# A hybrid mixer and product-key expert layer on one core: one-hot building paced by halves of first products, and a dense schedule with two blocks' sums resident in PSUM

## The chip, the core and the metric

The kernel runs on one core of one Trainium2 chip. The core's engines work side by side, each through a queue of its own in order: TensorE (PE in the profile, its weight loads PEld), VectorE (DVE), ScalarE (ACT), GpSimd (POOL) and SyncE (SP, which here only issues transfers). They are tied to each other by semaphores. The metric is the device time of one execution in microseconds (us); lower is better. Times of three runs stand beside one profiled execution, from which every duration is read.

## The reference, cut to what matters

One layer over 1024 tokens of width 1024. A front part (normalisation, input projection, an RG-LRU group and an S5 group, output projection) makes the residual stream h; the change does not touch it. The second half is the product-key expert layer:

```python
def block(xb):                                   # 128 tokens
    q = (xb @ wq).reshape(128, 8, 256)           # 8 heads
    s1 = einsum('thd,kd->thk', q[..., :128], k1) # 128 keys each
    s2 = einsum('thd,kd->thk', q[..., 128:], k2)
    v1, i1 = top_k(s1, 16); v2, i2 = top_k(s2, 16)
    cand = (v1[..., :, None] + v2[..., None, :]).reshape(128, 8, 256)
    sc, cidx = top_k(cand, 16)
    e = i1[cidx // 16] * 128 + i2[cidx % 16]     # one of 16384 experts
    g = softmax(sc)
    act = gelu(einsum('thkd,td->thk', u_tab[e], xb))
    return einsum('thk,thkd->td', g * act, v_tab[e])
h = h + block(...)
return rms_norm(h, normf_g)
```

## The kernel before

The 8 blocks of 128 tokens are treated in two ways.

**Three gathered blocks (5, 6, 7).** For each chosen expert one row of `peer_u` and later one row of `peer_v` is fetched by an indirect transfer that GpSimd issues (`ask`, L1257), and VectorE takes it in: a product with its sum for a row of u (`gather`, L1296; the profile's `row<-row,xg`), a multiply-add into `hb` for a row of v (L1310; `hb<-row,act,hb`). One block has 128 + 128 rows, so there are 768 rows in all, counted by `mg.units`. Eight buffers hold rows on the way. `finish` (L1315) normalises a gathered block behind its last row and stores it.

**Five dense blocks (0 to 4).** All 16384 experts are computed for these 640 tokens, 128 experts at a time, which is one *tile* j (128 tiles):
- *First product* (`first`, L1335): gelu(u_j x) for 640 tokens, as two halves of 320 tokens. A half is 8 x 3 matmuls into one PSUM bank (`ap`; every float32 operand is split into a high and a low part, hence three products) and one ScalarE gelu. The operands `uh` and `ul` of a tile are made by ScalarE and VectorE from the loaded `ur`. Each `uh`, `ul` has two buffers.
- *Weights* G: which experts a token chose, and with what weight. `topk` (L1109) finds on VectorE, for one block, the 16 best keys of each half and head, the 16 best sums, their softmax and the two indices. `build_g` (L1197) transposes these into `kt` and then, for each *group* of 4 tokens (32 groups a block, 160 in all), makes one-hots (`ohA` on VectorE; `ohB`, one quarter on VectorE and three on ScalarE), multiplies them on TensorE (`gp`), and copies the result to `gs` on ScalarE. Each 32 tokens `gs` (2 MB) is stored to DRAM as `G_d`.
- *Second product* (`second`, L1489): (G x gelu) times v_j, 24 matmuls for one block of 128 tokens and 4 tiles, or 6 for one block and one tile, in the order `hh vl`, `hl vh`, `hh vh` for each half of 512 columns.

**The stages of the second half.** (1) Queries, and the search for the gathered blocks. (2) The *building stage*: four Python generators are merged by `Merge.run` (L98). It keeps an estimated end time for each engine and thread and lets the thread with the earliest time emit next; a thread that yields a function waits until that is true. The threads are `build` (search and one-hots of one dense block after the other), `ahead` (L1408: the first products of 97 tiles, stored as `A_d` through three `hr` buffers), and the gathers, which may take in rows until 363 of them are done (`gate`, L1279, with `EARLY`). What the merge emits is one fixed order for each engine. (3) `prologue` (L1526), then the *dense stage* (`dense`, L1577): 32 chunks of 4 tiles, in an order that is written out by hand (`manual_schedule`). A chunk does the first product of one tile of the next chunk (the other three were made ahead and are loaded back as `hr`), and the second product of its own 4 tiles for all 5 blocks; on VectorE it splits and weighs the next tiles and takes in a share of the rows that are left. `rows_of(slot)` (L1483) puts that share at seven places, in the proportions `SLOTS`.

In a chunk before, VectorE's parts that the prediction speaks of are: `low_h` and `low_v` (L1383, L1387: the low parts `hl` and `vl` of a tile), `weigh` (L1368: `hr<-hr,gq`), `split_u` (`ul`), and `add` (L1497), which adds a finished pair of PSUM banks (`vp`) to a block's accumulator `acc`:

```python
def add(b, p_):
    V.tensor_tensor(acc[b], acc[b], p_.rearrange("p a b -> p (a b)"), ALU.add)
def pair():
    return ppv.tile([P, 2, 512], F32, name="vp", tag="vp")
```

PSUM has eight banks. In the dense stage two hold `ap`, two the sum of block 4 over all chunks (`total`), and four are two pairs for blocks 0 to 3. TensorE's order in a chunk is: both halves of the first product; block 0; block 1; then, tile by tile, blocks 2, 3 and 4. There are four adds in each chunk. `last` (L1660) finishes the last chunk and normalises the five blocks.

Of the kernel before, what the change touches and what calls it, by code (L numbers as in the profile page):

```python
# [18 lines left out]
P = 128  # L19
# [956 lines left out]
EARLY = 363  # L976


def peer(tc, a, cst, pools, h, nx, mg):
# [129 lines left out]
    def topk(b):  # L1109
# [52 lines left out]
        t1 = pk.tile([P, P], F32, name="t1", tag="t1")  # L1162
# [33 lines left out]

    def build_g(b):  # L1197
        i1, i2, g = yield from topk(b)
        p_ = pt("gt")
        for n, x in enumerate((i1, i2, g.rearrange("p h k -> p (h k)"))):  # L1200
            PE.transpose(p_[:, n * P:(n + 1) * P], x, ident)
        yield
        kt = pk2.tile([P, 5, P], F32, name="kt", tag="kt", bufs=1)
        V.tensor_copy(kt[:, 0:3], p_[:, :3 * P].rearrange("p (a b) -> p a b", b=P))
        V.tensor_scalar(kt[:, 3:5], kt[:, 1:3], -1.0, None, ALU.mult)
        if b == dblocks[-1]:
            mg.flag("k")
        yield
        last = None

        def flush():
            gs, t4, p_ = last
# [15 lines left out]
        for t4 in range(0, P, 4):  # L1228
# [15 lines left out]
            yield  # L1244
# [4 lines left out]
            last = gs, t4, p_  # L1249
            yield  # L1250
        flush()
        yield
# [26 lines left out]
    def gate():  # L1279
        return lambda: mg.units < (share[0] if share else EARLY)  # L1280

    held = []
# [125 lines left out]
    def ahead():  # L1408
        fetch_u()
        yield  # L1410
        while made[0] < NA:
# [38 lines left out]
    def build():  # L1450
        for b in dblocks:
            yield from build_g(b)
        mg.flag("g")

    pace[0] = PACE
    mg.add([(0.0, build()), (1.0, ahead())])
# [120 lines left out]
    def dense():  # L1577
# [3 lines left out]
        for c in range(nch):  # L1581
# [10 lines left out]
            if carry:  # L1592
                add(*carry)
# [14 lines left out]
            load_v(c + 1, 2)  # L1608
# [3 lines left out]

            if more:
                nx[0].turn()
# [3 lines left out]
            add(0, pr[0])  # L1618
            if not more:
                last(now, pr)  # L1620
                return
            rows_of(2)

            pr.append(pair())
            for jj, t in enumerate(now):
                second(pr[2], 2, t, jj == 0, jj == JC - 1)
                if jj == 0:
                    second(total, 4, t, c == 0, False)
                    add(1, pr[1])
                    nx[0].weigh()  # L1630
                    rows_of(3)
                    pr.append(pair())
                second(pr[3], 3, t, jj == 0, jj == JC - 1)
                if jj:
                    second(total, 4, t, False, False)
                if jj:
# [7 lines left out]
                    if jj == 3:  # L1644
                        weights(c + 2) if c + 2 < nch else None
                        add(2, pr[2])
# [10 lines left out]
            carry = 3, pr[3]  # L1657
            now = nx

    def last(now, pr):  # L1660
# [4 lines left out]
        def norm(b):  # L1665
# [6 lines left out]
            else:  # L1672
                for i in range(2):
                    xi = x[:, 512 * i:512 * i + 512]
                    V.tensor_tensor(xi, xi, total[:, i], ALU.add)
# [21 lines left out]
        next(g[0])  # L1697
        rows_of(2)
        p0 = pr[1]
        for b in (2, 3):  # L1700
            p_ = pair()
            for jj, t in enumerate(now):
                second(p_, b, t, jj == 0, jj == JC - 1)
            add(b - 1, p0)
# [8 lines left out]
        for _ in g[2]:  # L1713
            pass
# [95 lines left out]
```

## Time and profile before

| | |
|---|---|
| three runs | 2625.11 us median (2624.61 to 2631.12) |
| the profiled execution | 2620.74 us, its span 2619.0 us |
| busy over the span | PE 96%, DVE 90%, ACT 50%, POOL 43% |
| granted TensorE clock, mean | 0.985 |
| moved by the DMA engines | 753.31 MB, mean 288 GB/s |

The page cuts the span into 40 slices and gives a digit (tenths) of busy time for each:

```profile
## 2 busy tenths in 40 slices
PE   7998999998999999999999999999999999999997
PEld 6776889998999999999999888888888888888885
DVE  7898659998999999999999399999989999999997
ACT  6566434332683965938739643333444433333442
POOL 0000000343664756848547054555445555554551
```

A slice is 65 us. Slices 9 to 22 are the building stage: ACT swings between 3 and 9, since the one-hots of a block come in one burst and the search of the next block stands between two bursts. DVE is at 9 throughout but for one slice near the end (3), in which no row may be taken in any more. From slice 23 on the dense stage runs: PE at 9 in every slice. A busy PE is not PE at its peak, so the prediction goes by the distance from one start to the next, not by these digits.

### The profile page before, as it was taken

To read this page: it belongs to the slowest core of one execution; us is meant where nothing else is said; L and a number is where in the kernel's file an instruction comes from. 1 tells how busy PE (TensorE), PEld (TensorE's weight loads), DVE (VectorE), ACT (ScalarE), POOL (GpSimd) and SP (SyncE) were. 2 spreads that over 40 slices of the span, in tenths; PEclk is the share of its full clock that TensorE was granted. 3 is DMA by queue.
4 is the path that set the end of the run, shared out by engine and by line. 5 is a ranking of instruction groups with operands and counts; after the bars stand their busy time and mean duration, and the time that the engine had idled before them with its cause. 6 is when DMAs were issued, how large, how long until landed. Compare 5 with 4: busy or idle time off the path is not lost.

```text
span 2619.0 us, 40771 instructions
## 1 busy us (share of the span) xinstructions
PE 2503.9 (96%) x14623; PEld 2268.0 (87%) x14623; DVE 2365.3 (90%) x4556; ACT 1321.8 (50%) x2402; POOL 1130.8 (43%) x777
## 2 busy tenths in 40 slices
PE   7998999998999999999999999999999999999997
PEld 6776889998999999999999888888888888888885
DVE  7898659998999999999999399999989999999997
ACT  6566434332683965938739643333444433333442
POOL 0000000343664756848547054555445555554551
PEclk9999999999999999999999999999999999999999
DMA  5113124587899998999989899999989999999993
GB/s 183 30 43 108 61 91 137 189 287 285 305 394 310 360 388 307 397 344 349 399 297 377 277 336 343 346 343 342 342 321 346 344 342 341 343 347 341 340 339 132
DMA packets 302539, 753.31 MB, mean 288 GB/s; under 512 B 28928, under 2 KB 127424, under 8 KB 297600
## 3 DMA queue, kind: packets, MB, share of 16 engines
q0 software_dynamic: 110592, 402.70, 42.2%
q1 hardware_dynamic: 186048, 337.85, 36.4%
q10 hardware_dynamic: 5696, 10.15, 1.2%
q8 instruction: 115, 1.88, 0.3%
q14 instruction: 88, 0.72, 0.1%
HBM read 663.44 MB, written 85.98 MB: 286 GB/s over the span
## 4 chain that ended last, share of the span: by engine, by line
PE 62%; DVE 22%; DMA 7%; ACT 4%; issue 3%; ACTq 0%; SPq 0%; DVEq 0%
PE vp L146 26%; PE ap L146 17%; PE total L146 7%; PE qp L146 4%; DMA A_d<-aa 3%; PE gp L146 3%; PE wop L146 3%; DVE row L146 2%; DVE oh L146 2%; DVE ul L146 2%; DVE hb L146 2%; ACT ohB L146 1%; DVE ix L146 1%; DVE ci L146 1%; DVE v L146 1%
## 5 line engine op out<-in xcount | busy, mean ns | idle before, releaser
L1264 POOL DMA_INDIRECT row<-in_peer_u_dram,idx x384 | 564.8, 1471 | 958.5 <-DVE scv L146 471.0
L1264 POOL DMA_INDIRECT row<-in_peer_v_dram,idx x384 | 563.2, 1467 | 440.6 <-DVE hb L146 302.4
L146 PE MATMUL ap<-xDl,uh 128*128 128x320 f32 x2048 | 650.9, 318 | 14.3 <-ACT aa L146 12.0
L146 PE MATMUL ap<-xDh,ul 128*128 128x320 f32 x2048 | 642.8, 314 | 8.8 <-DVE ul L146 8.8
L146 PE MATMUL ap<-xDh,uh 128*128 128x320 f32 x2048 | 641.5, 313 | 0.0
L146 DVE SCALAR_TENSOR_TENSOR hb<-row,act,hb 128x1024 f32<-128x1024 f32 x384 | 491.5, 1280 | 4.6
L146 DVE CUSTOM_DVE_ANT_0 row<-row,xg 128x1024 f32<-128x1024 f32 x384 | 457.6, 1218 | 7.1 <-DMA row<-in_peer_u_dram,idx 6.6
L146 PE MATMUL vp<-vl,hh 128*128 128x512 f32 x1024 | 400.2, 391 | 9.4 <-DVE h L146 6.7
L146 PEld LDWEIGHTS ap<-xDl,uh 128*128 128x128 f32 x2048 | 390.4, 191 | 17.7 <-ACT aa L146 13.7
L146 PEld LDWEIGHTS ap<-xDh,ul 128*128 128x128 f32 x2048 | 390.5, 191 | 11.9 <-DVE ul L146 10.5
L146 PE MATMUL vp<-vh,hl 128*128 128x512 f32 x1024 | 400.2, 391 | 0.0
L146 PE MATMUL vp<-vh,hh 128*128 128x512 f32 x1024 | 399.0, 390 | 0.0
L146 PEld LDWEIGHTS ap<-xDh,uh 128*128 128x128 f32 x2048 | 389.8, 190 | 0.0
L146 ACT ACTIVATE gq<-gt 128x640 f32<-128x640 f32 x128 | 174.9, 1366 | 306.5 <-DVE hr L146 302.8
L146 PEld LDWEIGHTS vp<-vl,hh 128*128 128x128 f32 x1024 | 192.6, 188 | 50.4 <-DVE h L146 7.6
L146 PEld LDWEIGHTS vp<-vh,hh 128*128 128x128 f32 x1024 | 192.8, 188 | 40.9
L146 PEld LDWEIGHTS vp<-vh,hl 128*128 128x128 f32 x1024 | 192.5, 188 | 38.8
L146 ACT ACTIVATE ohB<-ohB,kt 128x128 f32<-128x128 f32 x480 | 205.3, 496 | 0.0
L146 ACT ACTIVATE aa<-ap 128x320 f32<-128x320 f32 x194 | 84.4, 436 | 237.2 <-PE ap L146 206.0
L146 PE MATMUL gp<-ohB,ohA 128*128 128x128 f32 x1280 | 183.7, 278 | 17.9 <-ACT gs L146 8.9
L146 DVE TENSOR_TENSOR h<-h,vp 128x1024 f32<-128x1024 f32 x128 | 155.7, 1217 | 48.8 <-PE vp L146 48.5
L146 PEld LDWEIGHTS gp<-ohB,ohA 128*128 128x128 f32 x1280 | 169.7, 192 | 22.2 <-ACT gs L146 9.7
(444 smaller groups left out, 4485.9 us busy)
## 6 DMA issues: line engine op xcount, KB each, us to landing
ur<-in_uT_dram SPq DMA_DIRECT2D x128, 512.0 KB, 6.6
vr<-in_peer_v_dram SPq DMA_DIRECT2D x128, 512.0 KB, 6.7
gt<-G_d SPq DMA_DIRECT2D x32, 1280.0 KB, 9.5
G_d<-gs SPq DMA_DIRECT2D x19, 2048.0 KB, 23.5
A_d<-aa SPq DMA_DIRECT2D x96, 320.0 KB, 7.5
hr<-A_d SPq DMA_DIRECT2D x96, 320.0 KB, 5.5
wqr<-in_wq_dram SPq DMA_DIRECT2D x31, 512.0 KB, 3.8
row<-in_peer_u_dram,idx POOLq DMA_INDIRECT x384, 7.4
```

Source lines behind the costliest of these rows:

```text
L146: return fn(*args, **kw)
L1264: G.indirect_dma_start(out=r, out_offset=None, in_=a["peer_v" if at >= P else "peer_u"], in_offset=bass.IndirectOffsetOnAxis(ap=idx[n][:, ...
```

## The change

**In the building stage** the search and the one-hots become two threads. `choose` runs `topk` for all dense blocks and, from the second block on, may take its k-th step only when so many groups are built; `kt` gets two buffers. `build` makes the groups of all blocks in one loop, and a group may be emitted only when the count of *steps* (halves of first products, counted in `ahead`) is at least 23 plus the groups built. Rows are tied to the same count: 64 at first (`FIRST`), then 1.55 more for each half, and 2.1 for each half in the last part (`STEP`). A scratch tile of the search (`t1`) now lies on `ri`.

**In the dense stage** blocks 3 and 4 both keep their sums in PSUM over all chunks (`total`, two pairs of banks), and one pair is left for blocks 0, 1 and 2. There are three adds in each chunk. TensorE's order becomes: first half of the first product; block 0; second half; block 1; then, tile by tile, blocks 3, 4 and 2. `SLOTS` changes, and `last` is rewritten.

```diff
-EARLY = 363
+FIRST, STEP, KT, LEAD = 64, (1.55, 2.1), 2, 23
...
-        t1 = pk.tile([P, P], F32, name="t1", tag="t1")
+        t1 = ri.bitcast(F32)
...
-    def build_g(b):
-        i1, i2, g = yield from topk(b)
...
+    kts, groups, steps = {}, [0], [0]
+
+    def choose():
+        for n, b in enumerate(dblocks):
+            steps = topk(b)
+            k = 0
+            while True:
+                try:
+                    next(steps)
+                except StopIteration as e:
+                    i1, i2, g = e.value
+                    break
+                k += 1
+                at = P // 4 * (n - 1) + k
+                yield lambda: groups[0] >= at
...
+            kts[b] = kt
+            mg.flag(f"k{b}")
+            yield
+        mg.flag("k")
+
+    def build():
...
-        for t4 in range(0, P, 4):
+        for b, t4 in [(b, t4) for b in dblocks for t4 in range(0, P, 4)]:
+            if t4 == 0:
+                if f"k{b}" not in mg.flags:
+                    yield f"k{b}"
+                kt = kts.pop(b)
+            yield lambda: steps[0] >= LEAD + groups[0] or "ahead" in mg.flags
...
-            yield
+            yield lambda: steps[0] >= LEAD + groups[0] + 1 or "ahead" in mg.flags
             for e in range(4):
                 PE.matmul(p_[:, e * P:(e + 1) * P], A[:, e], B[:, e], start=True, stop=True)
             if last:
                 flush()
-            last = gs, t4, p_
+            last = gs, b, t4, p_
+            groups[0] += 1
             yield
...
     def gate():
-        return lambda: mg.units < (share[0] if share else EARLY)
+        return lambda: mg.units < (share or allow)[0]
...
                 if n == 0:
                     fetch_u(NA + 1)
+                if n % 2 == 0:
+                    steps[0] += 1
+                    if steps[0] > LEAD:
+                        allow[0] += STEP[steps[0] > LEAD + (ND - 1) * P // 4]
                 yield
...
-    mg.add([(0.0, build()), (1.0, ahead())])
+    mg.add([(0.0, build()), (0.0, choose()), (1.0, ahead())])
...
-    total = ppr.tile([P, 2, 512], F32, name="total")
-    ppv = pools.open("ppv", bufs=2, space=PSUM)
+    total = {b: ppr.tile([P, 2, 512], F32, name=f"total{b}") for b in (3, 4)}
+    ppv = pools.open("ppv", bufs=1, space=PSUM)
...
-    SLOTS = (2.0, 3.3, 2.5, 1.4, 1.0, 1.0, 0.5)
+    SLOTS = (4.0, 2.7, 2.3, 1.5, 1.0, 1.0, 1.0)
...
             if carry:
-                add(*carry)
+                add(2, carry)
             now[3].low_h()
             load_h(c + 1, 3)
             rows_of(0)
             now[3].low_v()
             load_v(c + 1, 1)
+
+            p_ = pair()
+            for jj, t in enumerate(now):
+                second(p_, 0, t, jj == 0, jj == JC - 1)
             for _ in fs:
                 pass
-
-            pr = [pair()]
-            for jj, t in enumerate(now):
-                second(pr[0], 0, t, jj == 0, jj == JC - 1)
+            add(0, p_)
...
+            nx[0].turn()
+            p_ = pair()
             for jj, t in enumerate(now):
-                second(pr[1], 1, t, jj == 0, jj == JC - 1)
+                second(p_, 1, t, jj == 0, jj == JC - 1)
...
             for jj, t in enumerate(now):
-                second(pr[2], 2, t, jj == 0, jj == JC - 1)
+                for b in (3, 4):
+                    second(total[b], b, t, c == 0 and jj == 0, False)
                 if jj == 0:
-                    second(total, 4, t, c == 0, False)
-                    add(1, pr[1])
+                    add(1, p_)
                     nx[0].weigh()
                     rows_of(3)
-                    pr.append(pair())
-                second(pr[3], 3, t, jj == 0, jj == JC - 1)
-                if jj:
-                    second(total, 4, t, False, False)
+                    p_ = pair()
+                second(p_, 2, t, jj == 0, jj == JC - 1)
...
-            carry = 3, pr[3]
+            carry = p_
```

In `last` the order of TensorE becomes: block 0, block 3 (into its total), block 1, the first 512 columns of block 4, block 2, the other 512 columns of block 4; the add of block 1 stands in front of block 2, and blocks 4 and 2 are normalised last.

**VectorE in the building stage.** Before, between two groups of one burst (`ohA` opens a group; `hb<-row` and `row<-row` are rows taken in; `ci`, `scv`, `cd`, `ix`, `v`, `s` and `oh` are the search):

```order
L146 TENSOR_TENSOR ohA<-iota,kt 128x512
L146 TENSOR_SCALAR ohB<-iota,kt 128x128
L146 SCALAR_TENSOR_TENSOR hb<-row,act,hb 128x1024
L146 MAX_INDEX ix<-v,s 128x8
L146 SCALAR_TENSOR_TENSOR hb<-row,act,hb 128x1024
L146 TENSOR_TENSOR ul<-ur,uh 128x1024
L146 TENSOR_TENSOR ohA<-iota,kt 128x512
```

Of the change, between two groups of the second block:

```order
L146 TENSOR_TENSOR ohA<-iota,kt 128x512
L146 TENSOR_SCALAR ohB<-iota,kt 128x128
L146 MAX_INDEX ci<-scv,cd 128x8
L146 SCALAR_TENSOR_TENSOR hb<-row,act,hb 128x1024
L146 MATCH_REPLACE cd<-scv,cd 128x80
L146 MAX scv<-cd 128x8 x2
L146 MAX_INDEX ci<-scv,cd 128x8 x2
L146 MATCH_REPLACE cd<-scv,cd 128x80
L146 SCALAR_TENSOR_TENSOR hb<-row,act,hb 128x1024
L146 MAX scv<-cd 128x8
L146 TENSOR_TENSOR ohA<-iota,kt 128x512
```

The search of the next block has moved from between the bursts to between the groups. Over the stage the order holds, from the first group's `ohA` to that of group 144 (of 160): before 291 rows and 79 `ul`, now 264 rows and 75 `ul`, and in both the search of four blocks and 144 groups' one-hots. On TensorE 24 halves now stand before the first group's `gp` (17 before), and from there on exactly one half between two groups; before it is one group or two after each half within a burst and none between bursts. Up to the first `ohA` VectorE's order is the same in both.

**VectorE at the start of a dense chunk.** Before, in the part of the stage where rows of v are taken in (`h_2452`, `h_2453`, `h_2450` are the accumulators of blocks 2, 3 and 0):

```order
L146 SCALAR_TENSOR_TENSOR hb<-row,act,hb 128x1024
L146 TENSOR_TENSOR h_2452<-h_2452,vp 128x1024
L146 TENSOR_TENSOR vl<-vr,vh 128x1024
L146 TENSOR_TENSOR h_2453<-h_2453,vp 128x1024
L146 TENSOR_TENSOR hl<-hr,hh 128x640
L146 SCALAR_TENSOR_TENSOR hb<-row,act,hb 128x1024 x2
L146 TENSOR_TENSOR vl<-vr,vh 128x1024
L146 SCALAR_TENSOR_TENSOR hb<-row,act,hb 128x1024 x4
L146 TENSOR_TENSOR ul<-ur,uh 128x1024
L146 TENSOR_TENSOR h_2450<-h_2450,vp 128x1024
```

Of the change, at the same place of a chunk:

```order
L146 SCALAR_TENSOR_TENSOR hb<-row,act,hb 128x1024
L146 TENSOR_TENSOR vl<-vr,vh 128x1024
L146 TENSOR_TENSOR h_2452<-h_2452,vp 128x1024
L146 TENSOR_TENSOR hl<-hr,hh 128x640
L146 SCALAR_TENSOR_TENSOR hb<-row,act,hb 128x1024 x4
L146 TENSOR_TENSOR vl<-vr,vh 128x1024
L146 TENSOR_TENSOR h_2450<-h_2450,vp 128x1024
L146 SCALAR_TENSOR_TENSOR hb<-row,act,hb 128x1024 x3
L146 TENSOR_TENSOR ul<-ur,uh 128x1024
L146 SCALAR_TENSOR_TENSOR hb<-row,act,hb 128x1024 x3
L146 TENSOR_TENSOR h_2451<-h_2451,vp 128x1024
```

One add is gone, the add of block 2 now waits for the last matmuls of the chunk before, and four rows (in all chunks of the change; two or three before) stand between it and the `vl` of the chunk's fourth tile.

**TensorE behind block 0 of a chunk.** The numbers tell the PSUM tiles apart. Before, block 1 follows in another pair:

```order
L146 MATMUL vp_16682<-vl_16652,hh_16607 128x512
L146 MATMUL vp_16682<-vh_16609,hl_16639 128x512
L146 MATMUL vp_16682<-vh_16609,hh_16607 128x512
L146 MATMUL vp_16724<-vl_16533,hh_16503 128x512
L146 MATMUL vp_16724<-vh_16505,hl_16526 128x512
```

Of the change, the second half of the first product follows:

```order
L146 MATMUL vp_16590<-vl_16586,hh_16538 128x512
L146 MATMUL vp_16590<-vh_16540,hl_16570 128x512
L146 MATMUL vp_16590<-vh_16540,hh_16538 128x512
L146 MATMUL ap_16615<-xDl_3339,uh_16358 128x320
L146 MATMUL ap_16615<-xDh_3338,ul_16359 128x320
```

Block 0 has moved forward by one half of a first product, so its fourth tile is reached after 24 + 18 matmuls of the chunk instead of 48 + 18.

More of the change, by code (lines that the diff above doesn't have):

```diff
@@ L1607, in dense @@
                 next(su)
-            load_v(c + 1, 2)
+            if not more:
+                last(now)
+                return
             rows_of(1)
@@ L1611, in dense @@
                 u = next(su)
-            if more:
-                nx[0].turn()
-            pr.append(pair())
+            load_v(c + 1, 2)
+            rows_of(2)
+            nx[0].turn()
+            p_ = pair()
             for jj, t in enumerate(now):
-                second(pr[1], 1, t, jj == 0, jj == JC - 1)
[L1618 to L1624, printed above, removed]
+                second(p_, 1, t, jj == 0, jj == JC - 1)
             for jj, t in enumerate(now):
-                second(pr[2], 2, t, jj == 0, jj == JC - 1)
+                for b in (3, 4):
+                    second(total[b], b, t, c == 0 and jj == 0, False)
                 if jj == 0:
-                    second(total, 4, t, c == 0, False)
-                    add(1, pr[1])
+                    add(1, p_)
                     nx[0].weigh()
                     rows_of(3)
-                    pr.append(pair())
-                second(pr[3], 3, t, jj == 0, jj == JC - 1)
-                if jj:
-                    second(total, 4, t, False, False)
+                    p_ = pair()
+                second(p_, 2, t, jj == 0, jj == JC - 1)
                 if jj:
@@ L1643, in dense @@
                     rows_of(3 + jj)
-                    if jj == 3:
-                        weights(c + 2) if c + 2 < nch else None
-                        add(2, pr[2])
+                    if jj == 3 and c + 2 < nch:
+                        weights(c + 2)
                     nx[jj - 1].low_v()
@@ L1656, in dense, with last @@
                     nx[jj].high()
-            carry = 3, pr[3]
+            carry = p_
             now = nx
-    def last(now, pr):
+    def last(now):
         nf = rows.tile([P, D], F32, name="nf", tag="row")
@@ L1674, in norm @@
                     xi = x[:, 512 * i:512 * i + 512]
-                    V.tensor_tensor(xi, xi, total[:, i], ALU.add)
+                    V.tensor_tensor(xi, xi, total[4][:, i], ALU.add)
                     V.tensor_tensor_reduce(sq[:, 512 * i:512 * i + 512], xi, xi, 1.0, 0.0, ALU.mult, ALU.add,
@@ L1697, in last @@
         next(g[0])
+        rows_of(1)
         rows_of(2)
[L1699 to L1704, printed above, removed]
-            next(g[b - 1])
-            for _ in g[b - 2]:
-                pass
-            p0 = p_
         for jj, t in enumerate(now):
-            second(total, 4, t, False, jj == JC - 1, (0,))
-        add(3, p0)
+            second(total[3], 3, t, False, jj == JC - 1)
+        add(3, total[3])
         next(g[3])
-        for _ in g[2]:
+        for _ in g[0]:
             pass
+        p_ = pair()
         for jj, t in enumerate(now):
-            second(total, 4, t, False, jj == JC - 1, (1,))
-        next(g[4])
-        next(g[3])
+            second(p_, 1, t, jj == 0, jj == JC - 1)
+        for jj, t in enumerate(now):
+            second(total[4], 4, t, False, jj == JC - 1, (0,))
+        add(1, p_)
+        next(g[1])
+        for _ in g[3]:
+            pass
+        next(g[4])
+        p_ = pair()
+        for jj, t in enumerate(now):
+            second(p_, 2, t, jj == 0, jj == JC - 1)
+        for jj, t in enumerate(now):
+            second(total[4], 4, t, False, jj == JC - 1, (1,))
+        for _ in g[1]:
+            pass
+        add(2, p_)
+        next(g[2])
+        next(g[2])
         next(g[4])
         next(g[4])
-        next(g[3])
+        next(g[2])
         next(g[4])
-        for n in (4, 3):
+        for n in (4, 2):
             for _ in g[n]:
```

26 lines of the change are left out of this document (10 added, 16 removed).

## The prediction

> **What bounds the kernel now.** I read the busy time by stages first, then the chain that ended last in order of time, then single instructions. The columns of the first view: busy us of PE, PEld, DVE, ACT and POOL, granted clock, DMA share, GB/s.
>
> ```profile
> 683.00:1437.00 754.00, 725.00 (x5118) 718.06 (x5117) 735.69 (x1759) 533.26 (x1309) 477.24 (x301) 0.99 0.98 355
> 1505.00:2574.00 1069.00, 1065.08 (x5209) 917.49 (x5208) 993.35 (x1085) 431.16 (x473) 556.60 (x397) 1.00 0.93 339
> ```
>
> The building stage (first row) has PE and DVE near their limit together; the dense stage (second row) has PE at its limit alone. The chain, as start, length and what, gives TensorE's prices:
>
> ```profile
> 905.21 1.78 PE gp L146 x16
> 906.99 3.52 PE ap L146 x24
> ...
> 1511.91 12.25 PE vp L146 x54
> ...
> 1676.35 7.04 PE ap L146 x48
> ...
> 1697.05 4.08 PE vp L146 x18
> ...
> 1710.65 7.04 PE ap L146 x48
> ...
> 1882.19 7.04 PE ap L146 x48
> ...
> 1922.31 7.04 PE ap L146 x48
> ```
>
> A half of a first product (24 matmuls) costs 3.52 us, a group (8 passes) 1.78/2 = 0.89, a matmul of the second product 4.08/18 = 0.227, so 24 of them 5.44. A dense chunk is 7.04 + 120 x 0.227 = 34.2 us, and the chunks come every 34.3 (1676.35 to 1710.65): nothing is lost there, but for one chunk of 40.1 (1882.19 to 1922.31), in which block 6 is finished. The first dense block starts at 1511.91, 7.04 behind the end of the 194 halves made ahead: they end at 1504.9. So the time is 1504.9, then 32 chunks, then the end.
>
> **The building stage.** How much of it is VectorE's work? Where it starts the first group and group 144 (DVE, start and length), and what it waits for in between (us in total, times, longest):
>
> ```profile
> 680.86 0.68 DVE L146 TENSOR_TENSOR ohA<-iota,kt 128x512 f32<-128x512 f32 x1
> ...
> 1413.98 1.22 DVE L146 TENSOR_TENSOR ul<-ur,uh 128x1024 fp32r<-128x1024 f32 x1
> 1415.12 0.69 DVE L146 TENSOR_TENSOR ohA<-iota,kt 128x512 f32<-128x512 f32 x1
> 1415.72 0.34 DVE L146 TENSOR_SCALAR ohB<-iota,kt 128x128 f32<-128x128 f32 x1
> 1415.97 0.69 DVE L146 TENSOR_TENSOR ohA<-iota,kt 128x512 f32<-128x512 f32 x1
> ```
> ```profile
> DVE ohA L146 <- PE gp L146: 11.3, 5, 4.6
> DVE ul L146 <- ACT uh L146: 4.5, 3, 2.2
> DVE row L146 <- DMA row<-in_peer_u_dram,idx: 2.2, 4, 0.9
> ```
>
> From 680.9 to 1416.0 are 735.1 us, with 18.0 of waits: 717.1 us of work. Instructions overlap a little, so I price them from start to start:
>
> ```profile
> 2032.55 1.22 DVE L146 CUSTOM_DVE_ANT_0 row<-row,xg 128x1024 f32<-128x1024 f32 x1
> 2033.70 0.08 DVE L146 DVE_READ_ACCUMULATOR2_ANT act<- 128x1 f32 x1
> ```
>
> A row of u costs 1.15 (2032.55 to 2033.70), a `ul` 1.14 (1413.98 to 1415.12). Between the same two groups the order of the change has 27 rows fewer (rows 326 to 352, all of u: 31 us) and 4 `ul` fewer (4.5); search and one-hots are the same. That leaves 717.1 - 35.5 = **681.6 us** of VectorE's work, from the same 680.9, since its order up to there is unchanged: it is done at 1362.5 if it never waits.
>
> TensorE alone would do it faster. In the change one half stands between two groups, 3.52 + 0.89 = 4.41. Some 17 halves are done when VectorE comes to 680.9; 177 x 3.52 + 160 x 0.89 = 765 would end at about 1449. From group 0, which waits for 24 halves (about 707), group 144 would come at 707 + 144 x 4.41 = 1342. VectorE gets there 20 us later, so **VectorE stays the bound** through the paced part, by about 0.15 us a group. Its lead of some 25 us from the 24 halves is eaten by the early search of block 1. Behind group 144 it has little left (rows stop), and TensorE sets the end: 1362.5, 1.0 for the two one-hots of DVE, 16 x 0.89 + 26 x 3.52 = 105.8, so 1469.
>
> To this come waits. For VectorE's I take 5 of the 18.0 of before: these stand where `G_d` stores of 2 MB come every 25 us in a burst, and the change spreads them to one in 8 groups, some 36 us. For TensorE behind group 144 I take 3. The 194 halves then end at **1477, 28 us earlier**. The ends: PE alone sets the pace (1451, a gain of 54), or the waits grow to 27 (1496, a gain of 9).
>
> What costs nothing: `t1` on `ri` and the second `kt` change no instruction. ScalarE's work per half stays (533 of 754 us busy above), and the rows' transfers only move.
>
> **The dense stage.** Removed are 31 adds of VectorE. What does VectorE wait for there, and what did an add cost? (First the waits in a stretch of 30 chunks, then one chunk before, which starts at 1710.49.)
>
> ```profile
> DVE h L146 <- PE vp L146: 45.3, 47, 2.0
> ```
> ```profile
> 1709.32 1.21 DVE L146 TENSOR_TENSOR h<-h,vp 128x1024 f32<-128x1024 f32 x1
> 1710.45 1.22 DVE L146 TENSOR_TENSOR vl<-vr,vh 128x1024 fp32r<-128x1024 f32 x1
> 1711.59 1.21 DVE L146 TENSOR_TENSOR h<-h,vp 128x1024 f32<-128x1024 f32 x1
> 1712.72 0.82 DVE L146 TENSOR_TENSOR hl<-hr,hh 128x640 fp32r<-128x640 f32 x1
> 1713.46 2.60 DVE L146 SCALAR_TENSOR_TENSOR hb<-row,act,hb 128x1024 f32<-128x1024 f32 x2
> 1715.97 1.22 DVE L146 TENSOR_TENSOR vl<-vr,vh 128x1024 fp32r<-128x1024 f32 x1
> 1717.11 5.28 DVE L146 SCALAR_TENSOR_TENSOR hb<-row,act,hb 128x1024 f32<-128x1024 f32 x4
> 1722.31 1.22 DVE L146 TENSOR_TENSOR ul<-ur,uh 128x1024 fp32r<-128x1024 f32 x1
> ...
> 1728.68 1.22 DVE L146 TENSOR_TENSOR h<-h,vp 128x1024 f32<-128x1024 f32 x1 [1.51 <-PE vp L146]
> ```
>
> An add costs 1.13, so 35 us leave VectorE, and some 22 rows (25 us) come in that the building stage no longer takes. Neither counts here by itself: TensorE sets the chunk, and VectorE already waits for it. What counts is where VectorE is late. Put times into a chunk that starts at 0:
> - TensorE, change: first half to 3.52, block 0 from there, its fourth tile at 3.52 + 18 x 0.227 = **7.60** (before: 7.04 + 4.08 = 11.1).
> - VectorE, change: the add of block 2 needs the last matmul of the chunk before. An add that waits starts 0.27 behind the next matmul's start (block 1 ended at 1710.49 + 17.92 = 1728.41; the add started at 1728.68). Then 1.13 for the add, 0.74 for `hl`, four rows of v 5.20 (1717.11 to 1722.31), `vl` 1.22: 0.27 + 1.13 + 0.74 + 5.20 + 1.22 = **8.56**. With rows of u it is 0.27 + 1.13 + 0.74 + 4 x 1.15 + 1.22 = 7.96.
>
> Before, this `vl` was done at 1717.19, 6.7 into the chunk and needed at 11.1: cover of 4.4 us, which the change uses up by moving block 0 forward (3.5) and adding rows. That TensorE does wait for just this `vl` is seen in the last chunk of before, which has no first product in front:
>
> ```profile
> 2580.85 0.50 PE L146 MATMUL vp<-vl,hh 128*128 128x512 f32 x1 [2.64 <-DVE vl L146]
> 2590.80 0.50 PE L146 MATMUL vp<-vl,hh 128*128 128x512 f32 x1 [2.82 <-DVE h L146]
> ```
>
> So TensorE waits 1.0 in a chunk with rows of v and 0.4 in one with rows of u, and VectorE can't make it up, since its add of block 2 waits for TensorE again. By 13.5 rows a chunk, 19 chunks are of v and 11 of u: 19 x 1.0 + 11 x 0.4 = 23.4, **24 us with what is rounded**. The ends: 0 (the low part comes in time) and 31 x 1.0 = 31.
>
> The other new waits are covered. Block 1 needs the add of block 0, which waits for the end of block 0 (9.96), is done by 11.5 and has the second half in front of it (to 13.5). Block 2 needs the add of block 1: it starts at 19.2 if VectorE is free, is done by 20.4, and is needed behind 12 matmuls into the resident sums (21.6). Behind an add that came late stand `weigh`, rows and the low parts of the next tiles. The chunk that finishes block 6 keeps its 5.9 us: its last rows, its square sum and the add of block 1 stand in the same order.
>
> **The end.** The last chunk begins with block 0 at once, so `vl` (8.6) is waited for longer than the 2.64 above, by about 2; the order behind it wins some back, and one add more stands in front of the two last normalisations: **+1 us**, between -2 and +5.
>
> **The sum.** Against the span of 2619.0: -28 + 24 + 1 = -3, so 2616. The profiled run took 2620.74, 4.4 below the median of 2625.11; I put the difference on the median: **2622 us**. A measurement of this kernel can tell some 0.3%, 8 us, from no change, and this is within it: what the building stage gains is spent in the dense chunks.
>
> **The clock.** A wait of TensorE may cost more than its length, as the chain shows behind two waits:
>
> ```profile
> 1906.81 0.57 PE L146 MATMUL vp<-vl,hh 128*128 128x512 f32 x1 [3.92 <-DVE h L146]
> ```
> ```profile
> 1906.81 5.98 PE vp L146 x18
> ...
> 2590.80 11.22 PE vp L146 x48
> ```
>
> Behind 3.92 us of idle, 18 matmuls took 5.98 instead of 4.08: 1.9 us more. Behind 2.82 us of idle, 48 took 11.22, 0.234 each: nearly full speed. Waits of 1.0 us are well below both, so I add nothing. The Trainium skill, page "TensorE: Matmul & The Clock Gate", section "HAM oscillation — how this bites in real kernels", puts the danger at idle gaps of more than about 3.4 us, and the two rows agree. Its section "A second HAM failure mode: psum-queue depth-cycling" speaks against this change: cycling through PSUM lets TensorE idle briefly between groups of matmuls so often that the clock goes back and forth. By the first rule the sum stays; by the second it is the third rival below.
>
> **The rivals.**
> 1. *The low part comes in time* (faster). If the four rows run quicker, or the fourth tile is reached later, the 24 us fall away: 2622 - 24 = 2598. For it: only 0.4 to 1.0 us a chunk decide. Against: the same chain of five instructions stands in the rows above, and none of them waited. Chance 0.19.
> 2. *TensorE sets the pace of the building stage* (faster): a gain of 54 instead of 28, 2596. For it: VectorE is only 0.15 us a group too slow. Against: its 681.6 us are a difference of two counts and hardly uncertain. Chance 0.12; both together, 2572, 0.04.
> 3. *The clock falls at each wait* (slower): 31 x 1.9 = 59 us more, 2681. For it: 31 waits where there were none. Against: the 2.82 us row. Chance 0.04.
> 4. *Stores hold up ScalarE* (slower). The stores of `G_d` and `A_d` share SP's queue, and ScalarE cannot write a new `aa` until its store has landed:
>
> ```profile
> ACT aa L146 <- DMA A_d<-aa: 30.8, 6, 8.6
> ```
>
> Six of 20 stores cost 5 us each, all in bursts; DMA's share in this stage is 0.98. If the shorter stage keeps the queue from draining, so that each of 18 stores costs VectorE, the bound, 1.5 us more, 27 us come on top: 2649. It decides for slower from 0.6 us a store. Against: 36 us between stores instead of 25. Chance 0.15.
> 5. *The change doesn't do what it says:* the sums are resident, but the one pair makes TensorE wait in each chunk for the add of block 1 too, where only 1.2 us of cover stand: 1 us late is 31 us, 2653. Chance 0.04.
>
> My forecast keeps 0.42. **Range:** 2594 to 2650 takes in the forecast with its bounds, rivals 1 and 2 and most of 4; left out are both gains together (0.04), 3 and 5 (0.08) and part of 4 (0.05). Faster by over 0.3%: 0.19 + 0.12 + 0.04 = 0.35; within it 0.42; slower 0.15 + 0.04 + 0.04 = 0.23.
>
> **What would show it.** In the profile of the change: the first `vp` of the dense stage at about 1481 (1477 + 3.5; there is now one half in front); between the first group and group 144 VectorE busy without a break and short waits of PE for `ohA`, `ohB` or `ul`; in the dense stage a wait PE `vp` <- DVE `vl` about 30 times, near 1.0 us while rows of v are taken in and 0.4 for rows of u, and chunks of 35.3 and 34.7 us. Wrong would be: no such waits, chunks of 34.3, PE without gaps in the building stage, or long waits of ACT `aa` for `A_d`.

## The result and the profile after

| | median (lowest to highest) | runs | ratio to the kernel before |
|---|---|---|---|
| before | 2629.26 us (2624.61 to 2632.1) | 5 | |
| after | 2656.09 us (2654.03 to 2672.02) | 5 | 1.0117, 95% interval 1.009 to 1.0143 |

The change makes the kernel slower by 1.2%; 2622 was forecast. One execution of kernel 2 below, of 4974.23 us, and one of the kernel before, of 8713.06 us, are left out of all medians and ratios. The profiled execution of the change is the slowest of its five, 15.9 us above their median. It reaches the first group at 694.10, 13.2 us later than the profiled execution of before (680.86), with one wait of VectorE of 13.1 us for `S_d` ahead of it; this wait is 0 to 4.2 us in ten of the profiled executions of this study and 12.2 to 13.8 in the other four. So stages are compared by their lengths, not by their places.

First the two stretches that answer to those shown of before (from the first group to group 144, and thirty dense chunks). The columns are those of the prediction: stretch and length, busy us of PE, PEld, DVE, ACT, POOL, granted clock, DMA share, GB/s.

```profile
694.10:1398.50 704.40, 672.73 (x4781) 665.50 (x4781) 681.05 (x1668) 521.92 (x1259) 420.34 (x265) 0.99 0.97 345
1530.00:2591.00 1061.00, 1038.69 (x5022) 883.45 (x5021) 953.00 (x1062) 416.38 (x456) 563.22 (x407) 1.00 0.94 341
```

VectorE's work up to group 144 is 681.05 us; 681.6 was predicted. But the stretch took 704.4, where 686.6 was predicted with the waits, and the stage as a whole, from the first group to the end of the 194 halves (1523.8, which is 3.5 ahead of the first dense block at 1527.3), took 829.7 us, where before took 823.8 and the prediction had 796. What was waited for in the building stage (us in total, times, longest):

```profile
ACT aa L146 <- DMA A_d<-aa: 41.8, 4, 15.6
DVE ul L146 <- ACT uh L146: 41.4, 8, 12.1
PE ap L146 <- ACT aa L146: 28.4, 8, 10.3
```

ScalarE waits for a store of `A_d` to land (30.8 us in six waits before, 41.8 in four now), and TensorE and VectorE wait for ScalarE. All four stand behind 1300. One of them in single instructions (start, length, and in brackets the idle time and what ended it):

```profile
1354.60 0.44 ACT L146 ACTIVATE aa<-ap 128x320 f32<-128x320 f32 x1 [15.61 <-DMA A_d<-aa]
1355.09 0.64 PE L146 MATMUL ap<-xDl,uh 128*128 128x320 f32 x1 [10.31 <-ACT aa L146]
1358.84 1.23 DVE L146 TENSOR_TENSOR ul<-ur,uh 128x1024 fp32r<-128x1024 f32 x1 [10.07 <-ACT uh L146]
```

The queue of SyncE ahead of it (start, and how long the issue took):

```profile
1318.49 0.37 SPq L1235 DMA_DIRECT2D G_d<-gs  x1
1320.84 24.19 SPq L1449 DMA_DIRECT2D A_d<-aa  x1
1345.13 0.44 SPq L1351 DMA_DIRECT2D ur<-in_uT_dram  x1
```

Here an `A_d` store that stands behind the 2 MB of a `G_d` store holds the queue for 24 us, and the next loads with it. Why here and not earlier in the stage? The windows (same columns):

```profile
1100.00:1200.00 100.00, 97.42 (x697) 95.94 (x695) 100.00 (x275) 76.56 (x188) 56.11 (x34) 1.00 0.95 327
1250.00:1300.00 50.00, 47.24 (x342) 46.86 (x342) 49.16 (x88) 37.85 (x90) 40.99 (x26) 1.00 1.01 375
1300.00:1350.00 50.00, 40.12 (x278) 39.55 (x277) 42.91 (x76) 27.03 (x68) 36.09 (x28) 0.94 1.04 408
1350.00:1400.00 50.00, 44.91 (x305) 44.91 (x306) 38.64 (x66) 37.16 (x93) 30.40 (x23) 0.89 1.02 391
```

Up to 1200 VectorE is full and the DMA engines move 327 GB/s. From 1300 to 1400 no computing engine is full, and the DMA engines are: share 1.02 to 1.04, 391 to 408 GB/s. POOL's column tells whose transfers come on top: it issues the rows, 34 in 100 us at first, 28 in 50 us later. The last search has ended by then (at 1214.5), VectorE is free for rows, and in VectorE's order 78 of them stand between groups 112 and 144, where the 32 groups before have 51.

The dense stage, by its waits in the second stretch (the first row is TensorE's weight loads, which come ahead of its matmuls):

```profile
PEld vp L146 <- DVE vl L146: 27.0, 29, 2.3
PE vp L146 <- DVE vl L146: 14.8, 19, 1.8
PE vp L146 <- DVE h L146: 6.3, 1, 6.3
```

and one chunk, VectorE from the add of block 2 on, and TensorE's fourth tile:

```profile
1736.40 1.22 DVE L146 TENSOR_TENSOR h<-h,vp 128x1024 f32<-128x1024 f32 x1 [0.15 <-PE vp L146]
1737.54 0.82 DVE L146 TENSOR_TENSOR hl<-hr,hh 128x640 fp32r<-128x640 f32 x1
1738.28 5.24 DVE L146 SCALAR_TENSOR_TENSOR hb<-row,act,hb 128x1024 f32<-128x1024 f32 x4
1743.43 1.22 DVE L146 TENSOR_TENSOR vl<-vr,vh 128x1024 fp32r<-128x1024 f32 x1
1744.71 0.50 PE L146 MATMUL vp<-vl,hh 128*128 128x512 f32 x1 [0.67 <-DVE vl L146]
```

These are the predicted five instructions with `vl` last and TensorE waiting for it. The price of the wait is read from the distance of the chunks: they come every 35.3 us with rows of v and every 34.8 with rows of u (34.3 before). From the end of the halves to the end of the kernel it is 1146.4 us; before, 1114.3.

### The profile page after: what moved, and what is told of

Same layout as the page of the kernel before. It is cut to its first block, busy times and chain, and to the rows that moved or that the text cites. A ratio compares the mean times of both kernels' runs of the same rounds, so it can differ in the third digit from the quotient of the medians.

```text
span 2670.2 us, 40637 instructions
## 1 busy us (share of the span) xinstructions
PE 2517.5 (94%) x14623; PEld 2267.4 (85%) x14623; DVE 2334.8 (87%) x4525; ACT 1332.8 (50%) x2402; POOL 1127.3 (42%) x777
## 5 line engine op out<-in xcount | busy, mean ns | idle before, releaser
L1287 POOL DMA_INDIRECT row<-in_peer_u_dram,idx x384 | 557.2, 1451 | 978.8 <-DVE scv L146 471.6
L146 PE MATMUL vp<-vl,hh 128*128 128x512 f32 x768 | 304.9, 397 | 27.8 <-DVE vl L146 18.9
L146 PE MATMUL vp<-vh,hl 128*128 128x512 f32 x768 | 301.6, 393 | 0.0
L146 PE MATMUL vp<-vh,hh 128*128 128x512 f32 x768 | 299.6, 390 | 0.0
L146 PEld LDWEIGHTS vp<-vl,hh 128*128 128x128 f32 x768 | 144.3, 188 | 70.5 <-DVE vl L146 31.9
L146 DVE TENSOR_TENSOR ul<-ur,uh 128x1024 fp32r<-128x1024 f32 x128 | 156.5, 1223 | 54.4 <-ACT uh L146 54.2
L146 PE MATMUL total<-vl,hh 128*128 128x512 f32 x512 | 200.4, 391 | 0.0
L146 PE MATMUL total<-vh,hl 128*128 128x512 f32 x512 | 200.3, 391 | 0.0
L146 PE MATMUL total<-vh,hh 128*128 128x512 f32 x512 | 200.0, 391 | 0.0
L146 ACT ACTIVATE ha<-ap 128x320 f32<-128x320 f32 x62 | 27.1, 437 | 345.8 <-PE ap L146 345.8
```

The source lines that it names most:

```text
L146: return fn(*args, **kw)
L1287: G.indirect_dma_start(out=r, out_offset=None, in_=a["peer_v" if at >= P else "peer_u"], in_offset=bass.IndirectOffsetOnAxis(ap=idx[n][:, ...
```

## The experiments

Each was timed in five rounds beside the kernel before, whose median was 2621 to 2631 us in these jobs; single runs of that kernel scatter by 10 us and more either way, so the ratios are compared. A stage's length is from the first group to the end of the halves, in the profiled execution.

**1 and 2: each half of the change alone.** Kernel 1 (e1) keeps the building stage of the change and puts the dense stage of before behind it; kernel 2 (e2) the other way round. (The expectations name kernels by labels, e1 to e13; there is no e6.)

```diff
 e1_build_only, against the change
-    total = {b: ppr.tile([P, 2, 512], F32, name=f"total{b}") for b in (3, 4)}
-    ppv = pools.open("ppv", bufs=1, space=PSUM)
-    SLOTS = (4.0, 2.7, 2.3, 1.5, 1.0, 1.0, 1.0)
+    total = ppr.tile([P, 2, 512], F32, name="total")
+    ppv = pools.open("ppv", bufs=2, space=PSUM)
+    SLOTS = (2.0, 3.3, 2.5, 1.4, 1.0, 1.0, 0.5)
...
 e2_dense_only, against the change
-FIRST, STEP, KT, LEAD = 64, (1.55, 2.1), 2, 23
+EARLY = 363
...
```

> The building stage of the change with the dense stage of before. Theory A (the dense part costs what its profile shows: 1.0 us a chunk with rows of v, 0.46 with rows of u, 24 us; the chunk that finishes block 6 3.6 more; the end 3; together 31 us, all of the measured loss, and the building stage gives nothing): 0 us against before, within 6. Theory B (the building stage loses the 19 us of the one profiled run): 15 to 20 us slower than before. Theory C (the building stage gains the 28 us of the prediction in most executions): 25 us faster.

> The building stage of before with the dense stage of the change. Theory A: 28 to 32 us slower than before, waits of PE vp for DVE vl of 0.7 us or so in chunks with rows of v, chunks of 35.3 and 34.8 us. Theory B: 12 us slower. Theory C: 50 us slower or more (the dense part must then cost what the building stage gains on top of the measured loss).

Measured: kernel 1 2629.11 us, ratio 1.0013 (0.9993 to 1.0033); kernel 2 2647.49 us, ratio 1.0081 (1.0049 to 1.0112), which is 21 us. The dense half costs about what was predicted (in the profile, from the end of the halves on, 1139.3 us against 1114.3, 25 more). The building half, 28 us in the forecast, gives nothing in the time, and 4 us in the profile: 819.9 us against 823.8.

**3: the rate of rows.** The second rate of the change, 2.1 rows for each half, brought down to the first.

```diff
-FIRST, STEP, KT, LEAD = 64, (1.55, 2.1), 2, 23
+FIRST, STEP, KT, LEAD = 64, (1.55, 1.55), 2, 23
```

> The change with 1.55 rows for each half to the end instead of 2.1 in the last part: 24 rows fewer in the building stage, 24 more in the dense one. If the rows' rate in the last part is what fills the DMA engines and holds up the stores (waits of ACT aa for A_d 42 us): these waits fall below 15 us, the building stage ends 20 us earlier, the dense stage grows by some 6 us (0.2 rows more in front of vl in each chunk): 10 to 15 us faster than the change. If the rate doesn't matter: the waits stay, and it is 5 us slower than the change.

Measured: 2659.69 us, ratio 1.0138 (1.0108 to 1.0167). The rate is not where the crowd comes from: VectorE's order has the same 325 rows ahead of group 144, since the scheduler pulls all rows that may be taken into VectorE's free places. But behind group 144 hardly any is left, since 329 rows may be taken in instead of 352, and the stage is 810.5 us, the shortest so far: 698.7 to group 144, as in kernel 1, and 111.8 behind it, near the 109.8 of the forecast. The dense stage lost it again: 23 rows more stand there, up to five ahead of `vl`, and its chunks are up to 38.2 us.

**4: the shared queue.** `G_d` stores issued by ScalarE instead of SyncE.

```diff
-                    nc.sync.dma_start(G_d[js, :, t0:t0 + GT].rearrange("j p t q -> p j (t q)"),
+                    nc.scalar.dma_start(G_d[js, :, t0:t0 + GT].rearrange("j p t q -> p j (t q)"),
```

> The change with the stores of G_d issued by ACT instead of SP, so that no A_d store and no load stands behind them in SP's queue. If the shared queue is the cause: no wait of ACT aa for A_d over 2 us, the paced part runs to the end as VectorE's work allows, the building stage ends 20 to 35 us earlier than in the profiled run of the change, and it is 15 to 30 us faster than the change. If the DMA engines themselves are full: the waits stay, no change within 5 us. If ACT is held up by its own stores: idle of ACT in front of ohB, slower.

Measured: 2659.75 us, ratio 1.0127 (1.0096 to 1.0157). No wait for `A_d` is left, and the stage is 821.8 us all the same. Its waits and its window from 1300 on:

```profile
ACT gs L146 <- DMA G_d<-gs: 23.6, 3, 10.9
PE ap L146 <- DVE ul L146: 19.7, 13, 2.8
```
```profile
1300.00:1350.00 50.00, 46.30 (x316) 45.74 (x315) 43.68 (x76) 31.37 (x77) 35.99 (x26) 0.93 1.05 407
```

Now the `G_d` stores themselves land too late for their two buffers. In this kernel the queue decides who waits, not how much: the DMA engines are as full as in the change (1.05 of their time). The Trainium skill, page "DMA: Bandwidth & Descriptors", section "Issuing engines are not separate DMA queues", says that transfers started by several engines run on the same 16 DMA engines and interleave. This run agrees.

**5: the low part first.** In each dense chunk `vl` of the fourth tile is made ahead of the rows of slot 0.

```diff
-            rows_of(0)
             now[3].low_v()
             load_v(c + 1, 1)
+            rows_of(0)
```

> The change, with the low part vl of the fourth tile put ahead of the rows of slot 0 in each dense chunk. Theory A (the dense part loses its time at this low part): vl is then done at 0.27 + 1.13 + 0.74 + 1.22 = 3.4 us into the chunk and needed at 7.6, so the waits PE vp <- DVE vl (about 21 us in the change) fall under 4 us and chunks become 34.3; the time falls by 20 to 26 us against the change (2656), to 2630 to 2636, ratio to the kernel before about 1.002. Rival (the single pair of banks is what binds): the waits move to PE vp <- DVE h, the adds now standing behind rows, chunks stay at 35 us and the time at 2650 or more. The building stage stays as in the change under both.

Measured: 2627.68 us, ratio 0.9993 (0.9976 to 1.0011). The wait for `vl` is gone from the dense chunks, which come every 34.4 us, and nearly all of the dense stage's loss with it: 1115.6 us from the end of the halves, where before has 1114.3 and the change 1146.4. VectorE in one chunk:

```profile
1682.99 1.22 DVE L146 TENSOR_TENSOR h<-h,vp 128x1024 f32<-128x1024 f32 x1 [0.15 <-PE vp L146]
1684.13 0.82 DVE L146 TENSOR_TENSOR hl<-hr,hh 128x640 fp32r<-128x640 f32 x1
1684.86 1.22 DVE L146 TENSOR_TENSOR vl<-vr,vh 128x1024 fp32r<-128x1024 f32 x1
1686.00 5.24 DVE L146 SCALAR_TENSOR_TENSOR hb<-row,act,hb 128x1024 f32<-128x1024 f32 x4
```

One pair of PSUM banks for three blocks is enough: no other wait took its place. TensorE's only wait for VectorE in thirty chunks is 5.3 us for an add, in the chunk that finishes block 6.

**6 to 9 (e7 to e10): the same rows, spread.** From the last search on the instructions keep the order in which they are emitted, so rows stay at their places: 261 ahead of group 128 instead of 282, 294 ahead of group 144 instead of 325, and 352 in all as in kernels 1 and 5. Kernel 6 does it to kernel 1, kernel 7 to kernel 5.

```diff
-    mg.run([], until="g")
+    with tc.manual_schedule():
+        mg.run([], until="g")
```

> Building stage of the change with the dense stage of before (as in e1_build_only), and from the last search on the instructions keep the order in which they were emitted: 261 rows stand ahead of group 128 and 294 ahead of group 144, where e1 has 282 and 325. Rows in all, stores and TensorE's order are the same. Theory B (rows that crowd in front of group 144 fill the DMA engines to some 405 GB/s from 1250 to 1420, so the stores of A_d and G_d land late and ScalarE, then TensorE and VectorE wait): DMA share falls below 1.0 there, ACT aa <- DMA A_d from 33 to under 10 us, and from the first group to the end of the halves 790 to 800 us instead of 819.9; time 2600 to 2612, ratio about 0.993. Rival (the order on SP's queue, a G_d store ahead of an A_d store, or the transfers of the block that is finished there, are enough by themselves): aa waits of 25 us or more stay, and the time stays at 2625 to 2632.

> The change with both edits: vl ahead of the rows of slot 0 and the emitted order kept from the last search on. If theories A and B both hold, their gains add: 2656 - 23 - 25 = 2608, between 2598 and 2616, and the dense stage is no faster than that of before (its chunks are 34.3 at best). If only A holds 2633; if only B holds 2631; if neither, 2650 or more.

Measured: 2707.47 us, ratio 1.0298 (1.0269 to 1.0327), and 2704.71 us, ratio 1.0282 (1.0252 to 1.0313): a miss that says nothing of rows. The scheduler had also issued the loads of `ur` early, and that went too (kernel 6, from 1250 to 1600):

```profile
ACT uh L146 <- DMA ur<-in_uT_dram: 121.0, 19, 16.3
```

So kernels 8 (from kernel 6) and 9 (from kernel 7) issue these loads up to two tiles ahead:

```diff
-            nextu.append(load_split(pu, a["uT"][order[made[0] + len(nextu)]], [8, P], "u"))
+            for k in range(i, min(i + 3, NA + 1)):
+                if k not in raws:
+                    raws[k] = pu.tile([P, 8, P], F32, tag="raw", name="ur", bufs=3)
+                    nc.sync.dma_start(raws[k], a["uT"][order[k]])
...
```

> As e7_kept_order (building stage of the change, dense stage of before, emitted order kept from the last search on), but the loads of the raw first operands (ur) are issued up to two tiles ahead; e7 had lost that lead, and its ScalarE waited 4 to 16 us for ur. 261 rows ahead of group 128 and 294 ahead of group 144 (e1: 282 and 325). Theory B (crowded rows fill the DMA engines, stores land late): no ur waits of several us, aa waits for A_d under 10 us in all, DMA under 390 GB/s from 1250 on, from the first group to the end of the halves 790 to 805 us (e1 819.9); time 2603 to 2615, ratio about 0.994. Rival (SP's queue order alone makes the waits): aa or uh waits stay near 25 us, time 2625 or more.

> The change with vl ahead of the rows of slot 0 (as e5, 2628), the emitted order kept from the last search on, and the ur loads two tiles ahead. Theory B: the building stage gains 15 to 25 us on e5, so 2603 to 2613, faster than both kernels; the dense stage as in e5 (chunks of 34.3, 1112 us from the first second product on). Rival: 2625 or more, as e5.

Measured: 2626.84 us, ratio 1.0008 (0.9993 to 1.0022), and 2623.66 us, ratio 0.999 (0.9975 to 1.0005). Both are half a miss. Against kernels 1 and 5 they carry two edits, the kept order and the early loads. In kernel 8 the waits for `A_d` fall from 33.2 to 4.8 us, and group 144 comes 681.0 us after the first instead of 699.1. Then it is all given back: from there to the end of the halves 138.6 us instead of 120.8, and the stage is 819.6 again. Where (windows of kernel 8, then its waits from group 144 on):

```profile
1250.00:1300.00 50.00, 48.45 (x352) 48.26 (x351) 32.85 (x60) 38.60 (x93) 15.90 (x12) 1.00 0.78 260
1300.00:1350.00 50.00, 50.00 (x364) 50.00 (x363) 40.55 (x71) 36.86 (x93) 31.06 (x24) 1.00 1.04 397
1400.00:1450.00 50.00, 43.03 (x294) 42.80 (x294) 38.32 (x65) 26.53 (x64) 32.92 (x23) 0.93 0.98 361
1450.00:1500.00 50.00, 34.30 (x214) 33.77 (x213) 20.40 (x25) 17.54 (x24) 9.85 (x9) 0.83 0.93 344
```
```profile
ACT vh L146 <- DMA G_d<-gs: 19.2, 1, 19.2
PE ap L146 <- ACT aa L146: 15.7, 2, 14.1
DVE row L146 <- DMA row<-in_peer_u_dram,idx: 11.4, 4, 9.0
```

The rows that were moved back meet the last `G_d` stores and the first loads of the dense stage, and now ScalarE waits 19.2 us for `G_d`. The bytes stayed: 277 MB in the stage in kernels 1, 5, 8, 9 and in the change, by the trace's count, in 820 to 830 us.

**10 and 11 (e11, e12): fewer rows.** The second rate at 1.2, so 314 rows ahead of the dense stage instead of 352; by the trace's count the stage moves 262 MB instead of 277. Kernel 10 does it to kernel 9, kernel 11 to kernel 5.

```diff
-FIRST, STEP, KT, LEAD = 64, (1.55, 2.1), 2, 23
+FIRST, STEP, KT, LEAD = 64, (1.55, 1.2), 2, 23
```

> e10_vl_preload (2624) with the second rate of rows at 1.2 instead of 2.1 for each half: 314 rows instead of 352 before the dense stage, so 20 MB less through the DMA engines in the building stage and 38 rows more (44 us of VectorE) in the dense stage, where VectorE of e5 waits about 40 us for TensorE's adds. Theory C (in every variant so far the building stage, from the first group to the end of the halves, moved 268 to 287 MB in 810 to 830 us; spreading the rows moved the waits, since the bytes stayed): about 350 GB/s without the 20 MB, 790 to 800 us, waits of the last part below 10 us, dense stage within 5 us of e10; time 2597 to 2608, faster than both kernels. Rival 1 (waits come from the order on SP's queue, whatever the bytes): 2618 to 2626. Rival 2 (the dense stage has no room for 38 rows): its chunks lengthen by about 1 us, 2625 or more.

> e5_vl_first (2628) with the second rate of rows at 1.2: 314 rows before the dense stage, in the scheduler's own order (282 ahead of group 128, 314 ahead of group 144, none behind). Theory C: the crowd up to group 144 stays (first waits of ScalarE for A_d, about 20 us, stay), the last one and those behind group 144 go: 2612 to 2620. Rival 1: 2626 to 2630. If crowding is of no account and bytes alone count: as e11.

Measured: 2600.66 us, ratio 0.9927 (0.9909 to 0.9946), and 2607.49 us, ratio 0.9945 (0.9925 to 0.9966). **Both beat both kernels.** The stages are 807.6 and 805.7 us, and the dense stage takes the 38 rows for nothing (1112.3 and 1111.8 us from the end of the halves; 1118.3 and 1115.6 in kernels 9 and 5). Kernel 11 came out below the 2612 to 2620 us expected, and not where it was expected: 686.4 us to group 144 instead of the 705.9 of kernel 5, and 119.4 behind it instead of 120.4. Of kernel 10 behind the last search:

```profile
1300.00:1350.00 50.00, 50.00 (x366) 50.00 (x365) 30.72 (x53) 39.03 (x99) 14.73 (x13) 1.00 0.92 322
1350.00:1400.00 50.00, 50.00 (x364) 50.00 (x363) 32.93 (x59) 37.43 (x97) 17.01 (x15) 1.00 0.83 278
1450.00:1500.00 50.00, 40.66 (x243) 39.43 (x244) 24.00 (x30) 19.75 (x28) 5.64 (x3) 0.86 0.86 295
```

TensorE is full where it lost 5 to 10 us in 50 in the change. In the last row TensorE still loses 9 us; there ScalarE waits once for the last `G_d` store:

```profile
ACT vh L146 <- DMA G_d<-gs: 15.0, 1, 15.0
```

The expected 790 to 800 us were missed by 8 us.

**12 (e13): fewer rows in the old order.** The kernel before, 330 rows instead of 363.

```diff
-EARLY = 363
+EARLY = 330
```

> The kernel before, with 330 rows instead of 363 allowed ahead of the dense stage (EARLY), nothing else. Theory C (what the building stage must move, and the VectorE work that comes with it, sets its length in the old order too): 33 rows less are 17 MB and 38 us of VectorE (717 to 679), so from the first group to the end of the halves 795 to 805 us instead of 824, and 2600 to 2615, if the dense stage of before takes 33 rows more (it waited 45 us for adds in 30 chunks, so most should fit). Then the gain of e11 and e12 over before needs neither the tied order nor the resident sums. Rival (the tied order is what lets the stage shrink; in the old one the bursts of one-hots keep it long): 2618 or more.

Measured: 2622.85 us, ratio 0.9994 (0.9974 to 1.0013); the stage is 820.7 us against 823.8. A miss for the theory that bytes and VectorE's work alone set the stage. The rows left out turn into waiting: VectorE waits for TensorE's groups 26.2 us ahead of group 144, where it waited 11.3.

```profile
1350.00:1400.00 50.00, 49.33 (x352) 49.03 (x351) 38.16 (x65) 30.79 (x76) 19.15 (x14) 1.00 0.69 253
1400.00:1450.00 50.00, 50.00 (x373) 50.00 (x373) 21.67 (x39) 49.73 (x132) 0.00 (x0) 1.00 0.59 181
```

In the old order TensorE is full there, with DMA at 0.59 to 0.69. So, by one profiled execution of each, fewer rows shorten the stage by 16 and 21 us in the tied order (kernel 10 against 9, 11 against 5) and by 3 in the old one. The tied order is worth having, but it pays only with fewer rows.

## Why the prediction was wrong, step by step

- **VectorE's work, 681.6 us:** right; 681.05, and 680.8 in kernel 1. (In the sum for TensorE alone, 680.9 + 765 gives 1446, not 1449; the forecast doesn't rest on it.)
- **The waits of the building stage:** the step that failed. The prediction had "For VectorE's I take 5 of the 18.0 of before: these stand where `G_d` stores of 2 MB come every 25 us in a burst, and the change spreads them", 3 us for TensorE behind group 144, and under what costs nothing "the rows' transfers only move". They move to the one place where nothing holds them back. Between groups 112 and 144 come 78 rows of 0.53 MB (148.77 MB for 282 rows in the stage of kernel 1), the DMA engines are at 1.02 to 1.04 of their time, and stores land late. In kernel 1 that is 699.1 us to group 144 instead of 686.6, and 120.8 behind it instead of 109.8: 23.5 of the 28 us that were to be gained. Kernels 8 to 11 show that the rows are what costs: spread, the waits came elsewhere; left out, the ratio to the kernel before fell from 0.9993 to 0.9945 (kernels 5 and 11) and from 0.999 to 0.9927 (9 and 10), 13 and 17 us. The stage follows the number of rows let in: 820 to 830 us with 352 (kernels 1, 4, 5, 8, 9 and the change), 810.5 with 329 (kernel 3), 807.6 and 805.7 with 314.
- **Dense chunks, +24 us:** right. 35.3 and 34.8 us against 35.3 and 34.7; kernel 2 alone +25 us in its dense stage; kernel 5 takes 31 of the 32 us back with one line moved.
- **"The chunk that finishes block 6 keeps its 5.9 us":** wrong by a little. It took 44.7 us, 10.4 more than the others of before, so 4.6 more than it did (3.4 more in kernel 2): TensorE waits 6.33 us for an add instead of 3.92.
- **The end, +1 us:** right; the last chunk and what follows took 46.1 us against 45.0, if the chunk ahead of it took 35.3 and 34.3.
- **The rivals.** The fourth, stores that hold up ScalarE, named the wait that is seen (ACT `aa` for `A_d`) and gave 2649. Its mechanism, one queue for two kinds of stores and a small price on each of 18, is not what happened: kernel 4 parts the queues and is no faster, and the waits are four, long, and all behind the last search. The fifth, the single pair, fell with kernel 5. The third, the clock: chunks with waits of 0.5 to 1 us kept the full clock. These waits come once a chunk, some 35 us apart. By the Trainium skill, page "TensorE: Matmul & The Clock Gate", section "A second HAM failure mode: psum-queue depth-cycling", which the prediction weighed, the clock might have gone back and forth. The trace of the change shows no such thing in these chunks.

Of the 32 us that the dense stage of the profiled execution lost, 26 are waits for `vl` (2.1 in the first chunk alone), 4.6 the chunk of block 6 and 1.1 the end. The range held up to 2650; the time lies 6 us outside, since the forecast's own gain was missing in full.

What stays open: that rows left out shorten the stage is shown; that their bytes do it is argued. No kernel was made with the same work of VectorE and fewer bytes, so the two are parted only by the windows (VectorE at 38.32 of 50 us and DMA at 0.98 in kernel 8, in a stretch that still lost time). And full DMA engines do not cost time by themselves. In kernel 1 TensorE lost nothing in this window:

```profile
1350.00:1400.00 50.00, 50.00 (x366) 50.00 (x366) 47.71 (x84) 39.16 (x96) 39.90 (x29) 1.00 1.04 407
```

What decides, beside full DMA engines, whether a late store or load costs time was not tested. Why the old order fills TensorE behind group 128 without ending sooner was not followed further either.

## What to carry to other kernels

Where a change frees an engine that also paces transfers, count the bytes of the stretch in which it comes free, not only its time: the DMA engines may be what the engines wait for next, and they stand in no engine's busy column. A cap on a rate does not set an order while a scheduler is free to fill gaps; look at the order for where the work ends up. And what one instruction is late by under a tight hand-written order is mended by its place (here `vl` ahead of four rows), before anything bigger is undone.

## What the hardware showed that was not expected

- The DMA engines of this core moved no more than some 410 GB/s over any 50 us of these runs (408 in the change from 1300 to 1350, at a share of 1.04), with rows, loads and stores mixed. The Trainium skill, page "DMA: Bandwidth & Descriptors", section "Bandwidth", puts the ceiling at 435 GB/s and 16 MB transfers at 425. The mix here stays some 6% below that ceiling.
- In the change an issue on SyncE's queue took 0.4 us as a rule, but 2 to 25 us for the first transfer behind a 2 MB store, from the first such store on. Up to 1300 ScalarE did not wait for a store of `A_d` because of it. In kernel 4, where these stores have another queue, no issue of SyncE took over 2 us.
- Around TensorE's wait of 6.33 us in the change the record of the clock has 10.2 us at half, around one of 3.92 us before 3.4; around waits of 1 us none. The prediction read a gap of 2.82 us, in the row at 2590.80, as nearly harmless; around three other gaps of before, of 2.77, 2.83 and 2.78 us (ending at 960.99, 1185.52 and 1337.58), the record has 3.4 us at half each. So the agreement that the prediction saw in two rows does not hold for the whole trace.
- One wait for a load of `S_d` is 0 to 4.2 us in some profiled executions and 12.2 to 13.8 in others. It does not explain the scatter from run to run by itself: the profiled execution of kernel 12 has 13.8 us of it and took 2622.67 us, where its median is 2622.85. Not all kernels scatter alike: the six executions of kernel 10 lie within 3.3 us.
